# Normalised input of the next attention block: loads and gain products ahead of the block change, high and low parts at it

## The chip, the core and the metric

One core of a Trainium2 chip (trn2). The metric is the device time of one execution in microseconds (us). Engines by the profile's names: PE (TensorE; PEld is its weight load), DVE (VectorE), ACT (ScalarE), POOL (GpSimd) and SP (SyncE), whose queue issues most of the DMAs.

## The reference

One layer with two parallel head groups over 2048 tokens of 1024 features, all in float32:

```python
h = rmsnorm(x, norm_mix_g)             # x * rsqrt(mean(x^2)+eps) * g
proj = h @ w_in                        # columns: u_ssm | q | k | v
y_ssm = s5_mixer(u_ssm, ...)           # complex diagonal scan, GELU, GLU
y_att = chunked_attention(q, k, v, rel_bias)   # 64-frame chunks, 8 to the left
x = x + concat(rmsnorm(y_ssm), rmsnorm(y_att)) @ w_out
x = x + (silu(h2 @ w_gate) * (h2 @ w_up)) @ w_down   # h2 = rmsnorm(x)
return rmsnorm(x)
```

The change concerns `h`, the input of the q, k and v projections.

## The kernel before

The kernel holds activations transposed (features on partitions, tokens on the free axis). Every float32 operand of a product is split into a high part (rounded by a copy to the matmul type `F32R`) and a low part (the rest), and a product is three matmuls: high by high, high by low, low by high (`mm3`, L148).

The run has these stages by the spans of the profile: a prologue with the projection of the scan's input (to about 130 us), attention with the scan beside it (to about 775 us), the output projection, then gate, up and down of the feed-forward part (from about 1000 us to the end).

**Attention** (`att_phase`, L678) works in 4 blocks of 512 tokens (`NSB`, index `sb`). A block is 32 steps: 4 pairs of heads, 2 heads, 4 quarters of 128 queries. A step issues scores of one quarter (`sc`, then the biased row minimum on DVE, L857, and the exponential on ACT, L860), the transposes of the quarter two steps before (`pt`, with their high and low parts `pth` and `ptl`, L875 and L876), every fourth step the product with v (`pj`), and then advances a list of `Unit`s: generators with a first and a last step. The units carry everything else: the projections (`qk_unit`, L740, and `v_unit`, L790, with their results in `pf` and weights in `w`, three buffers), the scan (`ssm_unit`, L557), and the preparation of `h` for the next block (`hT_unit`, L710). With `g0 = 32 * sb` the first step of a block, `CUT` has the first projection of block `sb` begin at `g0 - 8`, and the last one of the block before, `qk_unit(sb - 1, 3)`, ends there. I call that point the block change; there are three.

**`hT_unit`** makes, for each of the 8 feature tiles `q`, the product of the loaded `x` with the gain (a scalar per partition) and with the reciprocal root of the token (`rsn`): L735, on DVE. Then come the high part (L736, a cast on ACT) and the low part (L737, on DVE). Tiles 0 to 2 have two sets of high and low buffers, the `x` in names such as `hi0x` marks the set of odd blocks. Tiles 3 to 7 have one set, so that their high parts can be written only when the last projection of the block before has read the old ones. Tiles 0 to 3 are loaded into `xt` (two buffers), tiles 4 to 7 in two pairs into `raw` (two buffers). In block 0 `raw` also takes the weights before they are split (L686 and L156); the split weights are stored to `wss` (L708) and read back by later blocks (L702).

Before the change, a first unit does tiles 0 to 2 from step `g0 - 12` to `g0 - 9`, its loads up to 2 steps earlier (`HTA`); a second does tiles 3 to 7, all three operations, from `g0 - 8` to `g0 - 6`, its loads 2 steps earlier (`HTS`, `HTP`).

**What sets the order.** PE's instructions stay in program order. On the other engines, SP's queue included, the framework's scheduler places the instructions when the program is built, by priorities and its own idea of durations; after that every engine works strictly in its list's order. So an operation can stand far from where the units put it.

**The scan** shares the stage. `ssm_unit` loads `U`, `Bst`, `Tm` and `Vm` (L564), multiplies `U` by `Bst` on PE (`pj`, copied out at L588), runs a chain of small operations on POOL (L602 to L605, then the carries L613 and L614), hands the states over by four DMAs on POOL's queue (`XG<-X`, L636), and PE multiplies `U` by `Tm` and `XG` by `Vm`. Its results go out at L649. There are 8 such groups. The other DMAs on SP that matter here are q and k copies (L779, L780, L785, L751), bias rows (L552, L553) and the attention output (L910).

At the end of a projection of q and k in block 0, DVE multiplies by the root (L770), ACT makes high parts (L777 for q, L782 for k) and DVE low parts (L778 for q, L783 for k).

Of the kernel before, what the change touches and what calls it, by code (L numbers as in the profile page):

```python
# [13 lines left out]
ALU = mybir.AluOpType  # L14
# [4 lines left out]
KT = D // P  # L19
# [8 lines left out]
NSB = SEQ // SB  # L28
# [9 lines left out]
SGB = 2  # L38
RA1, RA2 = 2, 12
QS = 4, 5, 6, 7, 0, 1, 2, 3  # L40
HTA = -12, -9
HTS = -8, -6
HTP = 2
PRO = 0, 0, 2, 2, 2, 2, 0, 0, 0
LIGHT = 0.8
SL = 1
# [2 lines left out]
DB, XB = 3, 2  # L49
# [47 lines left out]
def f32(ap):  # L97
    return ap.bitcast(F32)
# [302 lines left out]
def u_phase(k, ident, S, aw):  # L401
# [3 lines left out]
    with ExitStack() as cx:  # L405
# [113 lines left out]
        for n in range(1, NSB):  # L519
            last, b = BLOCKS[n - 1 : n + 1]  # L520
            prep(b)
            if n == 1:
                bias_corners(k, S["nba"])
                bias_rows(k, S, 0, S["nba"])
            pf = FBANKS[n]
            now = [group(b, 0, 0 in pf)]
            finish(last, held)
            long(1)
            if n == NSB - 1:
                att = att_phase(k, ident, S, aw, X[b], lambda: ST[b])  # L530
                next(att)
            for f in (1, 2):
                now.append(group(b, f, f in pf))
                if n > 1:
                    long(1)
            sums(b)
            held = now + [group(b, 3, 3 in pf)]
# [140 lines left out]
def att_phase(k, ident, S, aw, x0, roots):  # L678

    tc, nc, io, pfs = k.tc, k.nc, k.io, k.pfs  # L680
    with ExitStack() as cx:
# [28 lines left out]
        def hT_unit(sb, q0=0, q1=KT):  # L710
            hi, lo = hT.setdefault(sb, ([], []))
            ts = slice(sb * SB, (sb + 1) * SB)
            xts = {}

            def load(q, n=1):
                t = k.t(aw, "raw", [P, 1024], bufs=2) if n > 1 else k.t(aw, "xt", [P, SB], bufs=XB)
                nc.sync.dma_start(t[:].rearrange("p (q t) -> p q t", q=n), io["xt"][q * P : (q + n) * P, ts].rearrange("(q p) t -> p q t", p=P))
                for m in range(n):
                    xts[q + m] = t[:, m * SB : (m + 1) * SB]

            if q0 == 0:
                load(0)
                load(1)
            else:
                load(q0)
                for q in range(q0 + 1, q1, 2):
                    load(q, 2)
            for q in range(q0, q1):
                yield
                if q0 == 0 and q + 2 < q1:  # L730
                    load(q + 2)
                xt = xts[q]
                for v, n in zip(hT[sb], ("hi", "lo")):
                    v.append(k.t(aw, f"{n}{q}x" if q < DB and sb % 2 else f"{n}{q}", [P, SB], F32R)[:])
                nc.vector.scalar_tensor_tensor(xt, xt, k.gm[:, q : q + 1], S["rsn"][:, ts], op0=ALU.mult, op1=ALU.mult)  # L735
                nc.scalar.copy(hi[q], xt)  # L736
                nc.vector.tensor_tensor(lo[q], xt, f32(hi[q]), op=ALU.subtract)  # L737
            yield

        def qk_unit(sb, pr):  # L740
# [47 lines left out]
        QK_N = 1 + 2 * KT  # L788
# [142 lines left out]
        sp = tc.alloc_tile_pool(name="ssm", reuse_waits="tile", bufs=1)  # L931
        psum = cx.enter_context(tc.tile_pool(name="aps", bufs=1, space=bass.MemoryType.PSUM, reuse_waits="tile"))
        psum2 = cx.enter_context(tc.tile_pool(name="aps2", bufs=1, space=bass.MemoryType.PSUM, reuse_waits="tile"))
        units = []
        for sb in range(NSB):
            g0 = sb * 32
            C = CUT if sb < NSB - 1 else CUTL
            if sb > 0:
                if DB:
                    units.append(Unit(hT_unit(sb, 0, DB), 2 + DB, g0 + HTA[0], g0 + HTA[1], 2))  # L940
                units += [Unit(hT_unit(sb, DB), 2 + KT - DB, g0 + HTS[0], g0 + HTS[1], HTP), Unit(qk_unit(sb, 0), QK_N, g0 + C[0], g0 + C[1], 3, light=LIGHT)]
            units.append(Unit(v_unit(sb, 0), V_N, g0 + C[1], g0 + C[2], 2, light=LIGHT) if sb else Unit(v0, V_N, *V0, done=1))
            for gen, n, c in ((qk_unit(sb, 1), QK_N, 2), (qk_unit(sb, 2), QK_N, 3), (v_unit(sb, 1), V_N, 4), (qk_unit(sb, 3), QK_N, 5)):
                units.append(Unit(gen, n, g0 + C[c], g0 + C[c + 1], 2, light=LIGHT) if sb else Unit(gen, n + 1, C[c], C[c + 1], 4, light=LIGHT, mid=2))
# [772 lines left out]
```

## Time and profile before

| | |
|---|---|
| median of 3 runs | 2294.59 us (2293.13 to 2301.24) |
| the profiled execution | 2293.41 us, its span 2291.6 us |
| PE busy | 2172.1 us (95% of the span) |
| DVE, ACT, POOL busy | 1542.1, 1000.9, 359.2 us (67%, 44%, 16%) |
| mean granted PE clock | 0.978 |
| around the first block change (130 to 280 us) | PE busy 117.27 of 150 us, clock 0.90 |
| rest of attention (280 to 775 us) | PE busy 450.73 of 495 us, clock 0.96 |
| from 1000 us on | PE busy 1265.88 of 1292 us, clock 0.99 |

A row of the waits view reads "engine, line, releaser: us in total, times, longest us". A row of the timeline reads "start us, duration us, engine, line, operation, out<-in, count", and in brackets the idle time of that engine just before and what ended it. A row of the view by windows has the window, its length, then for PE, PEld, DVE, ACT and POOL the busy us and the instructions, the granted PE clock, the mean share of time in which the 16 DMA engines were busy, and GB/s.

### The profile page before, as it was taken

The numbers are of one execution on the slowest core, as the hardware profiler recorded it, in microseconds if no ns is written. First come the engines' busy times: TensorE is split into PE (matmuls) and PEld (weight loads), VectorE is DVE, ScalarE is ACT, GpSimd is POOL, SyncE is SP. The second block draws the span as 40 slices with busy tenths as digits, with TensorE's granted clock in tenths as the row PEclk, the third lists the DMA queues.
The fourth block names the chain that finished last, engine by engine and source line by source line (L and its number), as shares of the span: only waits on it lengthen the run. The fifth ranks groups of instructions, "written<-read, shape, count | busy, mean of one in ns | idle before, by whom it ended". The sixth has DMA issues, their size and how long they took to land.

```text
span 2291.6 us, 30320 instructions
## 1 busy us (share of the span) xinstructions
PE 2172.1 (95%) x10632; PEld 1828.7 (80%) x10632; DVE 1542.1 (67%) x2695; ACT 1000.9 (44%) x1654; POOL 359.2 (16%) x827
## 2 busy tenths in 40 slices
PE   8987799989987899999999999999999999999997
PEld 6776688888986688878888887888888878888886
DVE  7745565555545855876776668666656477788776
ACT  6445555455546652343333335333333343354322
POOL 2246645456641000000000000000000010000000
PEclk9999999999998999999999999999999999999999
DMA  8766777766644434854564557564423295465552
GB/s 292 241 219 225 227 236 193 190 181 191 191 120 143 161 111 146 284 176 145 162 200 165 198 184 261 184 198 161 167 87 121 84 397 196 165 212 193 207 188 74
DMA packets 214872, 428.34 MB, mean 187 GB/s; under 512 B 38848, under 2 KB 61424, under 8 KB 207616
## 3 DMA queue, kind: packets, MB, share of 16 engines
q1 hardware_dynamic: 207072, 401.49, 54.2%
q0 software_dynamic: 7648, 24.92, 3.2%
q8 instruction: 83, 1.36, 0.2%
q14 instruction: 69, 0.57, 0.1%
HBM read 286.86 MB, written 129.00 MB: 181 GB/s over the span
## 4 chain that ended last, share of the span: by engine, by line
PE 73%; POOL 8%; issue 6%; DVE 4%; DMA 3%; ACT 2%; SPq 1%; DVEq 0%; POOLq 0%; ACTq 0%
PE X L79 20%; PE ps L79 17%; PE Y L79 10%; PE big L79 9%; PE pf L79 5%; PE W L79 5%; PE pj L79 3%; POOL X L605 2%; POOL st L602 1%; POOL st L603 1%; POOL X L604 1%; POOL X L614 1%; POOL fx L613 1%; PE sc L79 1%; PE pt L82 1%
## 5 line engine op out<-in xcount | busy, mean ns | idle before, releaser
L79 PE MATMUL X<-hi,c 128*128 128x512 f32 x1408 | 451.6, 391 | 7.7 <-DVE c L156 5.4
L79 PE MATMUL ps<-hd,hd 128*128 128x512 f32 (+1 forms) x1968 | 428.2, 379 | 3.2 <-DVE hd L156 2.0
L79 PEld LDWEIGHTS ps<-hd,hd 128*128 128x128 f32 x1968 | 356.4, 188 | 73.4 <-DVE hd L156 2.7
L79 PEld LDWEIGHTS X<-hi,c 128*128 128x128 f32 x1408 | 265.6, 189 | 64.0 <-DVE c L156 6.3
L79 PE MATMUL X<-lo,c 128*128 128x512 f32 x704 | 275.1, 391 | 0.0
L156 ACT CAST hd<-hd 128x1536 fp32r<-128x1536 f32 (+1 forms) x106 | 147.3, 1394 | 232.8 <-DMA hd<-hq 165.5
L79 PE MATMUL Y<-hi,c 128*128 128x512 f32 x704 | 225.1, 390 | 1.9 <-DVE u L1396 1.9
L156 DVE TENSOR_TENSOR hd<-hd 128x1536 fp32r<-128x1536 f32 (+1 forms) x106 | 174.1, 1644 | 35.0 <-ACT hd L156 34.5
L156 DVE TENSOR_TENSOR c<-S,c 128x512 fp32r<-128x512 f32 x176 | 121.0, 688 | 100.6 <-ACT c L156 100.3
L1500 POOL DMA_DIRECT2D hd<-hq x7 | 5.3, 764 | 1133.4 <-PE X L79 1121.1
L1392 ACT COPY u<-X 128x512 f32<-128x512 f32 x132 | 77.5, 588 | 201.4 <-PE X L79 201.4
L156 ACT CAST c<-S 128x512 fp32r<-128x512 f32 x176 | 109.4, 622 | 119.8 <-PE Y L79 61.6
L79 PE MATMUL big<-m,woh 128*128 128x512 f32 x512 | 161.0, 396 | 0.0
L1534 DVE TENSOR_TENSOR acc<-acc,ps 128x512 f32<-128x512 f32 x196 | 130.4, 683 | 41.6 <-PE ps L79 41.4
L79 PEld LDWEIGHTS Y<-hi,c 128*128 128x128 f32 x704 | 132.8, 189 | 30.5 <-DVE u L1396 2.8
L79 PEld LDWEIGHTS X<-lo,c 128*128 128x128 f32 x704 | 132.9, 189 | 27.7
L79 PE MATMUL pf<-hi,w 128*128 128x512 f32 x416 | 150.1, 412 | 4.0 <-ACT hi L736 4.0
L156 ACT CAST c<-raw 128x512 fp32r<-128x512 f32 x132 | 82.3, 623 | 151.4 <-PE Y L79 68.5
L79 PE MATMUL Y<-lo,c 128*128 128x512 f32 x352 | 137.3, 390 | 0.0
L876 DVE TENSOR_TENSOR ptl<-pt,pth 128x640 fp32r<-128x640 f32 (+3 forms) x152 | 98.3, 647 | 45.9 <-ACT pth L875 44.4
L860 ACT ACTIVATE s<-s,mn 128x640 f32<-128x640 f32 (+4 forms) x128 | 98.0, 765 | 58.5 <-DVE mn L857 53.6
L875 ACT CAST pth<-pt 128x640 fp32r<-128x640 f32 (+3 forms) x152 | 83.8, 551 | 87.4 <-PE pt L82 82.5
(443 smaller groups left out, 4290.3 us busy)
## 6 DMA issues: line engine op xcount, KB each, us to landing
w<-wss SPq DMA_DIRECT2D x36, 1024.0 KB, 6.3
hq<-g SPq DMA_DIRECT2D x140, 256.0 KB, 2.1
hd<-hq SPq DMA_DIRECT2D x35, 768.0 KB, 4.4
hd<-wc SPq DMA_DIRECT2D x35, 768.0 KB, 5.9
raw<-in_w_gate SPq DMA_DIRECT2D x44, 512.0 KB, 3.7
raw<-in_w_up SPq DMA_DIRECT2D x44, 512.0 KB, 4.2
wc<-px SPq DMA_DIRECT2D x66, 256.0 KB, 3.4
wss<-w SPq DMA_DIRECT2D x12, 1024.0 KB, 4.9
```

The lines of the kernel that those rows point to most:

```text
L79: return self.tc.keep_in_program_order(self.tc.nc.tensor.matmul(*a, **b))
L82: return self.tc.keep_in_program_order(self.tc.nc.tensor.transpose(*a, **b))
L156: return nc.scalar.copy(hi, raw), nc.vector.tensor_tensor(lo, raw, f32(hi), op=ALU.subtract)
L602: eng.tensor_tensor(t[:, :, :, :n], src, ar, op=ALU.mult)
L603: eng.tensor_tensor(t2[:, :, :, :n], src[:, ::-1], aw, op=ALU.mult)
L604: eng.tensor_tensor(dst, dst, t[:, :, :, :n], op=ALU.add)
L605: eng.tensor_tensor(dst, dst, t2[:, :, :, :n], op=ALU.add)
L860: nc.scalar.activation(s[:, :nk], s[:, :nk], AF.Exp, bias=mn[:], scale=-1.0, accum_out=sums[sb, pr][:, hh, qp : qp + 1])
L875: nc.scalar.copy(pth[:, a:b, qp, :], pt[:, a:b, :])
L876: nc.vector.tensor_tensor(ptl[:, a:b, qp, :], pt[:, a:b, :], f32(pth[:, a:b, qp, :]), op=ALU.subtract)
L1392: nc.scalar.copy(u[:], ps[:])
L1534: V.tensor_tensor(a, a, ps[:], op=ALU.add)
```

## The change

The loads and the gain product of tiles 3 to 7 become a first half of `hT_unit(sb, 3)`, spread over steps `g0 - 13` to `g0 - 8` (`HTN`, loads one step earlier, so from `g0 - 14`). The second half, with the high and low parts alone, keeps `HTS`. Both halves are one generator, of which the first unit takes 6 pieces by `islice`. The unit of tiles 0 to 2 keeps its three operations but moves from `g0 - 12 .. g0 - 9` to `g0 - 16 .. g0 - 13`. Lines behind L720 move down: the product is L722, the high part L742, the low part L743, and the later lines of attention stand 6 further.

```diff
-HTA = -12, -9
+HTA = -16, -13
 HTS = -8, -6
-HTP = 2
+HTN = -13, -8
...
+            def norm(q):
+                nc.vector.scalar_tensor_tensor(xts[q], xts[q], k.gm[:, q : q + 1], S["rsn"][:, ts], op0=ALU.mult, op1=ALU.mult)
...
                 for q in range(q0 + 1, q1, 2):
                     load(q, 2)
+                for q in range(q0, q1):
+                    yield
+                    norm(q)
             for q in range(q0, q1):
                 yield
-                if q0 == 0 and q + 2 < q1:
-                    load(q + 2)
-                xt = xts[q]
+                if q0 == 0:
+                    if q + 2 < q1:
+                        load(q + 2)
+                    norm(q)
...
-                nc.vector.scalar_tensor_tensor(xt, xt, k.gm[:, q : q + 1], S["rsn"][:, ts], op0=ALU.mult, op1=ALU.mult)
-                nc.scalar.copy(hi[q], xt)
-                nc.vector.tensor_tensor(lo[q], xt, f32(hi[q]), op=ALU.subtract)
+                nc.scalar.copy(hi[q], xts[q])
+                nc.vector.tensor_tensor(lo[q], xts[q], f32(hi[q]), op=ALU.subtract)
...
+        hts = {sb: hT_unit(sb, DB) for sb in range(1, NSB)}
...
-                units += [Unit(hT_unit(sb, DB), 2 + KT - DB, g0 + HTS[0], g0 + HTS[1], HTP), Unit(qk_unit(sb, 0), QK_N, g0 + C[0], g0 + C[1], 3, light=LIGHT)]
+                units += [Unit(islice(hts[sb], 1 + KT - DB), 1 + KT - DB, g0 + HTN[0], g0 + HTN[1], 1), Unit(hts[sb], 1 + KT - DB, g0 + HTS[0], g0 + HTS[1]), Unit(qk_unit(sb, 0), QK_N, g0 + C[0], g0 + C[1], 3, light=LIGHT)]
```

What the scheduler makes of it: PE's and POOL's orders are the same but for buffer numbers. On DVE, ACT and SP the order changes at the first block change (block 0 to 1), and by a few places in the middle of block 1 (the early tiles of block 2). At the second and third block change only numbers differ: there the loads and products of tiles 3 to 7 stood well ahead of the change already.

Place 1 is DVE at the first block change, where the last projection of block 0 ends. `yt<-pf,rsn` is the root product of k, the `k_...` rows are k's low parts, on which the next scores of PE depend; the rows with `sc` are the score minima, `lo...` low parts of `h` for block 1. Before, from the last early product to k:

```order
L735 SCALAR_TENSOR_TENSOR xt_2599<-xt_2599,g_mix_86,rsn_92 128x512
L857 ISA s_2730,mn_2731<-sc_2727,nbb_1549 128x512
L857 ISA mn_2731 128x1
L876 TENSOR_TENSOR ptl_2687<-pt_2734,pth_2686 128x128
L737 TENSOR_TENSOR lo2x_2648<-xt_2599,hi2x_2647 128x512
L886 RECIPROCAL rs_2893<-sm_2369 128x8
L876 TENSOR_TENSOR ptl_2687<-pt_2734,pth_2686 128x128
L770 TENSOR_TENSOR yt_2750<-pf_2640,rsn_92 128x512
L783 TENSOR_TENSOR k_539_2535<-yt_2750,k_539_2535 64x512
L783 TENSOR_TENSOR k_542_2538<-yt_2750,k_542_2538 64x512
```

and now, where `lo_601` to `lo_626` are the tiles 3 to 7:

```order
L743 TENSOR_TENSOR lo_603_2796<-raw_2510,hi_602_2795 128x512
L863 ISA s_2734,mn_2735<-sc_2731,nbb_1549 128x512
L863 ISA mn_2735 128x1
L882 TENSOR_TENSOR ptl_2696<-pt_2738,pth_2695 128x128
L892 RECIPROCAL rs_2893<-sm_2373 128x8
L882 TENSOR_TENSOR ptl_2696<-pt_2738,pth_2695 128x128
L743 TENSOR_TENSOR lo_605_2800<-raw_2510,hi_604_2799 128x512
L776 TENSOR_TENSOR yt_2754<-pf_2653,rsn_92 128x512
L743 TENSOR_TENSOR lo_607_2804<-raw_2512,hi_606_2803 128x512
L743 TENSOR_TENSOR lo_626_2860<-raw_2512,hi_625_2859 128x512
L789 TENSOR_TENSOR k_549_2558<-yt_2754,k_549_2558 64x512
L789 TENSOR_TENSOR k_552_2561<-yt_2754,k_552_2561 64x512
```

The early product has left this place, and the five low parts of tiles 3 to 7 have come in, four of which stand ahead of k's low parts in these rows (the first, `lo_601`, is the row just above). Before, those five and the five products of their tiles stood 9 rows and more behind k's low parts.

Place 2 is ACT at the same point: `s` the exponential of the scores, `rb` the spread of the row sums, `k` the high parts of k, `hi...` high parts of `h` for block 1. Before:

```order
L736 CAST hi2x_2647<-xt_2599 128x512
L860 ACTIVATE s_2730,sm_2369<-s_2730,mn_2731 128x512
L875 CAST pth_2686<-pt_2734 128x128
L888 COPY rb_2895<-rs_2893 128x512
L782 CAST k_539_2535<-yt_2750 64x512
L782 CAST k_542_2538<-yt_2750 64x512
```

and now:

```order
L866 ACTIVATE s_2734,sm_2373<-s_2734,mn_2735 128x512
L881 CAST pth_2695<-pt_2738 128x128
L742 CAST hi_604_2799<-raw_2510 128x512
L742 CAST hi_606_2803<-raw_2512 128x512
L742 CAST hi_625_2859<-raw_2512 128x512
L894 COPY rb_2895<-rs_2893 128x512
L788 CAST k_549_2558<-yt_2754 64x512
L788 CAST k_552_2561<-yt_2754 64x512
```

Three casts of `h` (tiles 5 to 7) now stand ahead of `rb` and k; tiles 3 and 4 stand a few rows higher. Before, all five came behind the next two quarters' scores.

Place 3 is SP's queue in the 45 us ahead of the first block change: `raw<-in_w_qk` are the last weights of block 0, `wss<-w` stores of split weights, `w<-wss` weights of block 1's first projection, `y<-X` the results of the scan's first group, `U`, `Bst`, `Tm` and `Vm` the loads of its second group. Before, from the last store of weights to the second load of weights:

```order
L708 DMA wss_74<-w_2436 128x2048
L564 DMA Bst_2562<-bsts_70 128x512
L702 DMA w_2652<-wss_74 128x2048
L649 DMA y_65<-X_2491 16x4x256 x8
L910 DMA ya_s_66<-ya_2278 128x512
L564 DMA U_2553<-u_64 16x16x64 x8
L564 DMA Tm_2564<-kts_78 16x4x128 x8
L564 DMA Vm_2573<-vs_71 128x4x128
```

with the early tile `xt_2599`, the four q copies and `w_2654` behind. Now the same stretch, in two pieces; first ahead of the stores of `y`:

```order
L717 DMA xt_2403<-in_xt 128x512
L553 DMA nbb_1549<-nbs_69 64x576
L717 DMA xt_2508<-in_xt 128x512
L717 DMA raw_2510<-in_xt 128x2x512
L717 DMA raw_2512<-in_xt 128x2x512
L708 DMA wss_74<-w_2452 128x2048
```

and then behind them:

```order
L649 DMA y_65<-X_2514 16x4x256 x8
L916 DMA ya_s_66<-ya_2278 128x512
L564 DMA U_2577<-u_64 16x16x64 x8
L564 DMA Bst_2586<-bsts_70 128x512
L564 DMA Tm_2588<-kts_78 16x4x128 x8
L564 DMA Vm_2597<-vs_71 128x4x128
L785 DMA q2h_2556<-q2h_2556 64x512
L786 DMA q2l_2557<-q2l_2557 64x512
L785 DMA q2h_2559<-q2h_2559 64x512
L786 DMA q2l_2560<-q2l_2560 64x512
L702 DMA w_2661<-wss_74 128x2048
L702 DMA w_2663<-wss_74 128x2048
```

All loads of `h` for block 1 now stand ahead of the stores of `y`; the first load of weights for block 1 (`w_2661`) has moved from ahead of them to behind the q copies, and `Bst` from ahead of them to behind the eight loads of `U`.

## The prediction

> **What bounds the kernel now.** Nearly everything is PE: it is busy for 95% of the span, so a change to preparation can only win where PE stands still. I read the waits of PE first, around the first block change (165 to 300 us).
>
> ```profile
> PE pj L79 <- DMA XG<-X: 8.4, 1, 8.4
> PE pt L82 <- DVE ptl L876: 7.0, 6, 3.2
> PE pf L79 <- ACT hi L736: 4.0, 2, 3.1
> PE sc L79 <- issue: 3.9, 1, 3.9
> PE pj L79 <- DMA Tm<-kts: 1.9, 1, 1.9
> PE pf L79 <- DVE lo L737: 1.5, 2, 1.2
> ```
>
> Only the L736 and L737 rows, 5.5 us, are waits for `h`. (The `ptl` row is softmax's own.) They belong to this block change alone: over the whole span the same two rows read the same, number for number. What PE waits for at the other two changes is the low part of k:
>
> ```profile
> PE sc L79 <- DVE k L783: 4.1, 2, 2.2
> ```
>
> Then PE's timeline at the first change, for the places where it stands:
>
> ```profile
> 247.96 0.45 PE L79 MATMUL sc<-k,q2h 128*128 128x128 f32 x1 [3.93 <-issue]
> ...
> 248.93 0.78 PE L79 MATMUL pf<-hi0x,w 128*128 128x512 f32 x1
> ...
> 256.12 0.49 PE L79 MATMUL pf<-hi,w 128*128 128x512 f32 x1 [3.12 <-ACT hi L736]
> ```
>
> Four stops stand in a row: the scan's hand-over at 210 to 218 and its next loads at 235 (the XG and Tm rows above), k at 248, the new `h` from 253 on. The stop called "issue" is k: DVE's low parts of k start at 247.18 (row below), the first of the two ends 0.8 later, and the scores start at 247.96.
>
> The stops cost twice, because the granted clock falls behind them. By windows, with PE's busy time as the second number and the clock after POOL's column:
>
> ```profile
> 256.00:260.00 4.00, 2.02 (x4) 0.77 (x4) 3.90 (x5) 1.74 (x4) 3.84 (x6) 0.76 1.00 341
> 260.00:264.00 4.00, 3.54 (x9) 2.96 (x10) 3.28 (x5) 0.81 (x2) 3.69 (x9) 0.50 0.04 17
> 264.00:268.00 4.00, 4.00 (x24) 3.50 (x23) 2.28 (x6) 2.15 (x5) 3.37 (x16) 0.89 0.01 2
> ```
>
> At clock c, a busy time b would have been b times c at full clock. The loss is 2.02 x 0.24 + 3.54 x 0.50 + 4.00 x 0.11 = 2.7 us.
>
> **The change, part by part.** I take each term in PE's time, against the profiled execution (2293.41 us, of which 2291.6 us is its span; 1.2 us under the median of 2294.59).
>
> *The waits for `h` go.* Loads and products of tiles 3 to 7 move ahead of the change, and the casts and low parts now follow right behind the last reads of the old tiles, near 240 to 247 us by the order, when PE still waits for k. PE needs tile 3 only after 253. So 5.5 us of waiting and 2.7 us of slow clock go: **-8.2 us**. This is the certain part; what follows asks what is late next.
>
> *The k stop.* The same casts and low parts now stand ahead of k on ACT and DVE.
>
> ```profile
> 242.93 1.03 DVE L735 SCALAR_TENSOR_TENSOR xt<-xt,g_mix,rsn 128x512 f32<-128x512 f32 x1 [2.60 <-DMA xt<-in_xt]
> ...
> 245.81 0.68 DVE L770 TENSOR_TENSOR yt<-pf,rsn 128x512 f32<-128x512 f32 x1
> 247.18 1.60 DVE L783 TENSOR_TENSOR k<-yt,k 64x512 fp32r<-64x512 f32 x2 [0.69 <-ACT k L782]
> ```
>
> ```profile
> L736 ACT CAST hi<-raw x12: 604/617/621, 257.8 to 547.3; 128x512 fp32r<-128x512 f32 x12
> ```
>
> Before, DVE sat 2.60 us for a late load, then did 1.03 of product and a low part before it reached `yt` at 245.81, though PE's last product for it ended at 244.03 (247.96 - 3.93). Now DVE has, from 244.03, to wait 0.6 for the cast of tile 5, then does its low part, `yt`, two more low parts and the first k, some 0.69 each: 0.6 + 4 x 0.69 + 0.7 = 4.1 us, against 3.93. **+0.2 us**. The ends: -1.0 (the product was the delay, and the low parts hide in waits for ACT) and +1.9 (the three casts at 0.617 stand wholly in k's way). I take the sum by the rows.
>
> *The first weights of block 1* are no longer fetched at 209.73 but in the place of the second ones:
>
> ```profile
> 209.73 0.72 SPq L702 DMA_DIRECT2D w<-wss  x1
> ...
> 241.84 0.54 SPq L702 DMA_DIRECT2D w<-wss  x1
> ```
>
> The two loads of this stretch took this long from issue to landing:
>
> ```profile
> DMA to landing us min/median/max: 5.8/7.1/8.3
> ```
>
> 241.84 + 7.1 = 248.9, and the first product wants them at 248.93, or 249.8 with the two delays of 0.7 and 0.2 that I count here. **0 us**, from 0 (5.8) to +0.5 at 8.3 (250.1). The second weights are wanted one projection half later.
>
> *`Bst` behind eight loads of `U`.* Before, it was fetched 20 us ahead; the stop at 235 waited for the loads of `U`. Now it comes one place behind the last `U`, which is one issue of SP, some 0.5 us (0.54 in the row of 241.84), later, and is larger (KB each, then median us to landing):
>
> ```profile
> U<-u SPq DMA_DIRECT2D x64, 64.0 KB, 3.0
> ...
> Bst<-bsts SPq DMA_DIRECT2D x8, 256.0 KB, 3.9
> ```
>
> So the wait grows by 0.5 if it lands as fast as `U`, by 0.5 + 0.9 = 1.4 at the medians. DMAs are less busy there than on the mean; I take **+0.7 us**.
>
> *The first hand-over of the scan* (the stop of 8.4 us). POOL ends its chain at 211.3 us and the DMAs carry `XG`; their landing times in that window, and at the next hand-over, were
>
> ```profile
> DMA to landing us min/median/max: 2.3/4.6/6.6
> ```
>
> ```profile
> DMA to landing us min/median/max: 4.1/6.1/7.8
> ```
>
> Two things move. First, POOL is slowed while DVE reads two operands from SBUF:
>
> ```profile
> 206.26 1.06 POOL L614 TENSOR_TENSOR X<-X,fx 128x434 f32<-128x434 f32 x1
> ...
> 209.41 1.90 POOL L614 TENSOR_TENSOR X<-X,fx 128x434 f32<-128x434 f32 x1
> ```
>
> ```profile
> 208.81 1.60 DVE L156 TENSOR_TENSOR w<-raw,w 128x1024 fp32r<-128x1024 f32 x1
> ```
>
> The weight split of 1.60 us cost POOL 0.84. The order puts two products and two low parts of the early tiles (four of about 0.7 us) into POOL's last 8 us: 2.8 x 0.84 / 1.60 = +1.5 us. Second, the 1 MB of weights and `Bst` that were issued just ahead of the last `XG` are replaced by 1 MB in two `raw` loads; the last `XG` may then land as fast as the fastest, 6.6 - 2.3 = 4.3 us earlier, or no earlier at all. I take the two as balancing: **0 us**, from -4.3 to +1.5.
>
> The Trainium skill speaks against the change here: "SBUF — State Buffer", section "Who interferes with whom", has DVE instructions with two SBUF inputs lock out a GpSimd instruction that reads SBUF for their whole length. By it the four operations delay the hand-over by all of their 2.8 us, not 1.5, and the sum below would be -3.8 instead of -6.6. The POOL row above bears out the contention, but at 0.84 for 1.60 us, not one for one.
>
> *The second hand-over.* PE would come to it earlier:
>
> ```profile
> 285.35 1.21 POOL L636 DMA_DIRECT2D XG<-X  x2 [0.30 <-POOL X L614]
> ```
>
> ```profile
> 297.05 0.59 PE L79 MATMUL pj<-XG,Vm 128*128 128x256 f32 x2
> ```
>
> Now PE arrives at 297.05 and does not wait. It will arrive at 297.05 - 8.2 + 0.2 + 0.7 = 289.75. The chain behind `XG` starts from the loads at 235, so it moves by +0.7 alone; but it gets relief, since the block of products and low parts goes that keeps DVE busy for 3.90 of 4.00 us in the window from 256. A scan step on POOL, from one L602 to the next, took
>
> ```profile
> 252.81 0.47 POOL L602 TENSOR_TENSOR st<-X,a 128x128 f32<-128x128 f32 x1
> ...
> 254.87 0.88 POOL L602 TENSOR_TENSOR st<-X,a 128x128 f32<-128x128 f32 x1
> ...
> 261.79 0.56 POOL L602 TENSOR_TENSOR st<-X,a 128x16 f32<-128x16 f32 x1
> ```
>
> 2.06 us once and 6.92 for the next two: 2.8 us lost, of which I give back 0.5 for the low parts that now come at 245 to 247. The last `XG` was issued at 285.35 + 0.6; it will be 285.95 + 0.7 - 2.3 = 284.35, and lands 6.1 later at 290.45. PE waits **+0.7 us**. The ends: 0 if it lands in 4.1, and +4.7 with no relief and 7.8 (294.45).
>
> *The other two block changes:* order and waits the same, **0 us**, 0.5 either way for the few rows that moved inside block 1. Behind 300 us, POOL's chains, loads and hand-overs start from PE's own instructions, so the whole shift stays.
>
> The sum: -8.2 + 0.2 + 0 + 0.7 + 0 + 0.7 + 0 = **-6.6 us**, and 2293.41 - 6.6 = 2286.8 us.
>
> The clock term could be figured otherwise. "TensorE: Matmul & The Clock Gate", section "What's actually happening", in the Trainium skill, gives about 3.4 us of half clock after an idle window. One such period is an estimate of 1.7 us instead of my 2.7, so -5.6 in all; the rows above show more than 4 us at half clock, because the waits kept interrupting.
>
> **The rivals.**
>
> *The second hand-over takes it back.* For: the gain arises behind the point from which POOL's chain starts, and `XG` had landed between 289.4 and 293.8 by the rows. Against: the relief. With the wait of 4.7: -6.6 + 4.0 = -2.6, 2290.8 us.
>
> *The first hand-over gains too.* For: the weights' megabyte and `Bst` leave its way. Against: `raw` loads and the same store of split weights come instead. At -4.3: 2282.5 us.
>
> *Slower, by the scan.* POOL held for the full 2.8 us, and `XG` in a queue of loads at 8.3 instead of 6.6 (+1.7): the first hand-over is 4.5 us late; `Bst` adds 1.4; the chain has no relief and lands after 7.8, at 285.95 + 5.9 + 7.8 = 299.65 instead of being there before 297.05. Then PE loses 2.6 us, 2296.0 us. It decides from where delays less relief and landing exceed 297.05 - 285.95 = 11.1 us; by the rows taken above they are 4.5.
>
> *The stop only moves.* The change touches one block change of three, and even there the scores wait for k behind five casts and low parts (+1.9), then for weights (+0.5): -6.6 + 2.2 = -4.4, 2289.0 us; and if the k stop grew by what the `h` waits lose, nothing would be left. For: three casts and four low parts now precede k in the lists. Against: DVE is rid of a 2.60 us wait there.
>
> **How the numbers follow.** The forecast, -4 to -9, has 0.60; the second hand-over 0.15; the first one earlier 0.12; slower by the scan 0.08; the stop that moves 0.05. The range from 2281.0 to 2293.0 holds the forecast, the second hand-over, the moved stop and most of the first one earlier, and leaves out the slower case; its ends are the unknown first hand-over (-4.3) with a faster k (-1.0), and a second hand-over at its worst with k at its worst. 0.5% is 11.5 us, about what a measurement of this kernel can tell from no change. Faster by more than that needs the first hand-over and k at their good ends: 0.06. Slower by more: 0.02, the far end of the scan's case. Within: 0.92.
>
> **What would show it.** In the changed profile the wait of `pf` for the high and low parts of `h` should be gone, the stop behind the last projection of block 0 should stay near 4 us and end with k's low part, the clock from 256 us on should be full, and PE should come to the second hand-over about 7 us earlier with a wait of a us or so. Wrong: a wait of PE for `w<-wss`, a first hand-over outside 216 to 220 us, a k stop above 5 us, a second hand-over with over 3 us, or changed waits at the second and third block change.

## Result and the profile after

Before and after were timed in turns on the same chips: 2293.40 us before (median of 14 runs, 2288.73 to 2301.24), 2287.02 us after (14 runs, 2281.13 to 2291.83). The ratio is 0.9969, with a 95% interval from 0.9958 to 0.9981: **6.4 us less, 0.3%**. A second set of runs gave 0.9969 again (0.9955 to 0.9984), and the kernel before against itself 1.0004 (0.9989 to 1.0019). So the gain is real, though no larger than the spread of single runs. The forecast was 2286.8 us. Its sum was right; how the sum came about was not, as the traces show.

The profiled execution of after is its fastest run: 2281.13 us, 12.3 less than the profile of before. Behind 300 us two profiles of one kernel drift apart by several us (two of the kernel before by 2.6 at 300 us and 5.1 at 490 us), so I compare places, not spans. PE's waits between 165 and 300 us, in the view "engine, line, releaser: us in total, times, longest":

```profile
PE pt L82 <- DVE ptl L882: 6.2, 5, 3.2
PE sc L79 <- issue: 4.7, 1, 4.7
PE pj L79 <- DVE ptl L882: 4.7, 2, 3.2
PE pj L79 <- DMA XG<-X: 2.6, 1, 2.6
PE pj L79 <- DMA Tm<-kts: 2.0, 1, 2.0
```

The rows of `pf` for high and low parts are gone. But two more rows changed that the forecast had left nearly alone: XG fell from 8.4 to 2.6, and `pj` now waits for `ptl`. On PE's timeline after, the number in brackets is the idle time ahead:

```profile
213.24 0.67 PE L79 MATMUL pj<-XG,Vm 128*128 128x256 f32 x2 [2.58 <-DMA XG<-X]
...
231.70 2.04 PE L79 MATMUL pj<-U,Bst 128*128 128x256 f32 x4 [2.02 <-DMA Tm<-kts]
...
246.46 0.45 PE L79 MATMUL sc<-k,q2h 128*128 128x128 f32 x1 [4.67 <-issue]
...
286.67 0.69 PE L79 MATMUL pj<-ptl,v 128*128 128x384 f32 x1 [3.20 <-DVE ptl L882]
```

The `ptl` that PE waits for at 286.67 stands on DVE behind two products for block 2, which wait for their load (DVE's and SP's timelines):

```profile
284.53 1.62 DVE L722 SCALAR_TENSOR_TENSOR xt<-xt,g_mix,rsn 128x512 f32<-128x512 f32 x2 [4.39 <-DMA xt<-in_xt]
286.06 0.55 DVE L882 TENSOR_TENSOR ptl<-pt,pth 128x384 fp32r<-128x384 f32 x1
```

```profile
275.61 1.01 SPq L717 DMA_DIRECT2D xt<-in_xt  x2
```

These are the early tiles of block 2, some 115 us ahead of their use (PE's first product of block 2 starts at 390.50): their loads are issued at 275.61, and DVE's products start 8.9 us later.

**How far PE is ahead, place by place.** The scores `sc<-k,q2h` come in the same order in all kernels. For each I took the start of the same score row in two profiles; the difference to before is the shift. Its change over a stretch is what the stretch won (-) or lost (+), slow clock included. The stretches, by the times of before: A, 206 to 231, the first hand-over; B, 231 to 241, the stop for U, Tm and Bst; C, 241 to 252, the k stop; D, 252 to 267, the tiles of the new `h`; E, 291.7 to 299.9, the second hand-over. Each row is one profile.

| us | A | B | C | D | E |
|---|---|---|---|---|---|
| forecast | 0 | +0.7 | +0.2 | -8.2 | +0.7 |
| after | -2.9 | +1.7 | +1.5 | -8.5 | +4.1 |
| after, second profile | -3.8 | +3.9 | +0.8 | -8.8 | +2.8 |
| before, second profile | -0.4 | -0.1 | +0.8 | +1.2 | 0.0 |
| 1 early tiles only | -2.4 | -0.3 | -3.0 | +0.3 | 0.0 |
| 2 split products only | -1.1 | -0.3 | -0.5 | +0.5 | -0.7 |
| 3 two transfers back | -2.2 | -0.2 | -0.4 | -2.5 | -0.3 |
| 4 products behind ptl | -2.0 | +3.4 | +1.5 | -8.4 | +1.3 |
| 5 block 2 loads in order | -1.0 | +1.7 | +1.5 | -8.4 | -0.7 |
| 6 k first | -5.3 | +4.2 | -1.3 | -8.8 | +3.4 |
| 7 Bst first | -5.6 | +0.9 | +1.5 | -8.3 | +4.2 |
| 8 = 5 + 6 + 7 | -5.7 | +2.9 | -1.3 | -8.8 | +3.9 |
| 9 = 5 + 6 | -2.5 | +1.7 | -1.4 | -8.7 | +6.1 |
| 10 = 9, one weight load back | -3.1 | +3.1 | -1.3 | -8.8 | +0.1 |

### The profile page after: what moved, and what is told of

It reads as the page before. It is cut to its first block, busy times and chain, and to the rows that moved or that the text cites. A ratio compares the mean times of both kernels' runs of the same rounds, so it can differ in the third digit from the quotient of the medians.

```text
span 2279.4 us, 30314 instructions
## 1 busy us (share of the span) xinstructions
PE 2170.2 (95%) x10632; PEld 1828.3 (80%) x10632; DVE 1541.6 (68%) x2695; ACT 999.2 (44%) x1654; POOL 353.7 (16%) x827
## 4 chain that ended last, share of the span: by engine, by line
PE 65%; POOL 11%; issue 8%; DMA 7%; DVE 5%; ACT 2%; SPq 1%; POOLq 0%; DVEq 0%; ACTq 0%
PE X L79 20%; PE ps L79 17%; PE Y L79 10%; PE big L79 7%; PE W L79 5%; PE pf L79 3%; POOL X L605 2%; DMA acc<-x 2%; POOL X L604 2%; POOL X L614 2%; POOL st L602 2%; POOL fx L613 2%; POOL st L603 2%; PE pj L79 1%; DMA lo<-hc 1%
## 5 line engine op out<-in xcount | busy, mean ns | idle before, releaser
L882 DVE TENSOR_TENSOR ptl<-pt,pth 128x640 fp32r<-128x640 f32 (+3 forms) x152 | 98.2, 646 | 44.8 <-ACT pth L881 43.2
```

Of the source, the lines that this page charges most:

```text
L882: nc.vector.tensor_tensor(ptl[:, a:b, qp, :], pt[:, a:b, :], f32(pth[:, a:b, qp, :]), op=ALU.subtract)
```

## Experiments

The theory after reading the two traces: D is the change's own gain and belongs to the whole change; A comes from the DMAs beside the last XG; E is DVE's stand for the load of block 2. The rivals: A is POOL's chain or chance; E is the second hand-over itself, so that XG ends it whatever DVE does.

**Second profiles of both kernels** (no edit) separate chance from change.

> The changed kernel itself once more, for a second profile. By the theory three things recur to 0.5 us: no wait of pf for high and low parts of h, DVE's stand of 4.4 us ahead of the products at 280 to 285 with PE's wait of 3.2 us for ptl, and the stop ahead of the scores of block 1 of 4.7 us. Open is the first hand-over of the scan, where PE's wait fell from 8.4 to 2.6 and the shift went from -1.0 to -4.0 us: if the changed loads make it, it recurs (-3 against before); if it was the chance of POOL's chain that began 1.75 us earlier in that execution, the second profile has the wait at 4 to 8 us.

> The kernel before once more, for a second profile and as a measure of how far the comparison itself scatters: ratio 1.000 within 0.0015. Open is the first hand-over: four profiles of changed kernels have PE's wait for XG at 1.1 to 3.5 us against 8.4 in the one profile of before. If that is the change, 7 to 9 us recur here, with XG issued last near 211.6 and landed 6 us later; if the profile of before was the exception, 2 to 5 us are seen here.

All three local findings recurred: no wait for `h`, a stop of 4.71 us at k, and 3.26 us of PE for `ptl`. The wait for XG recurred too, 3.0 us after against 8.7 before. So the shorter wait in A is the work of the change. The second profile of before also says what it isn't (POOL's last XG issues, SP's load, and PE's row):

```profile
209.32 1.21 POOL L636 DMA_DIRECT2D XG<-X  x2 [0.30 <-POOL X L614]
```

```profile
209.35 0.55 SPq L702 DMA_DIRECT2D w<-wss  x1
```

```profile
218.00 1.19 PE L79 MATMUL pj<-XG,Vm 128*128 128x256 f32 x2 [8.70 <-DMA XG<-X]
```

POOL was 2.3 us earlier here than in the first profile (209.32 against 211.60), and PE went on at 218.00 instead of 218.44. POOL does not set this hand-over. XG lands 7.5 us after its last issue ended (218.00 - 209.32 - 1.21), beside 1 MB of weights issued at the same moment. Here and below, XG counts as landed when PE starts its first product, which waits for it.

The size of A is another matter: in the nine profiles of kernels with the whole change it reaches from -1.0 to -5.7. It goes with how long the clock stayed at half, by the clock records of the traces. Half clock lasted 10.24 us in this stretch in both profiles of before and in 5 (-1.0), 6.83 us in after, 4, 9 and 10 (-2.0 to -3.1), 3.41 us in the second profile of after, 6 and 8 (-3.8 to -5.7), and in 7 (-5.6) there was none. Experiment 2, whose wait for XG stayed, has -1.1 with 6.83 us. So about 1 us of A can come without any gain at XG.

**1. The early tiles alone**

An edit of the kernel before:

```diff
-HTA = -12, -9
+HTA = -16, -13
```

> The kernel before with one of the two halves of the change: the first three tiles of each block loaded and multiplied four steps sooner; tiles 3 to 7 as before. Theory: the waits for h belong to tiles 3 to 7, so they stay at 4 to 5.5 us with the slow clock behind them, and nothing of the 8.5 us is won between 252 and 263. The first hand-over of the scan gains only if the weight split and the weight load leave its way: by the order both stand where the changed kernel has them, so PE's wait for XG falls from 8.4 to about 3 us and the shift behind it is -3 to -5, of which the stops at 232 and 247 give back 2 to 4. In all 0 to -3 us, ratio 0.9987 to 1.000. Rival: the first hand-over gain needs the whole change (or was chance in the profile of before), then the wait for XG stays at 7 to 8 us.

0.9980 (0.9966 to 0.9993). Its waits:

```profile
PE pf L79 <- ACT hi L736: 3.5, 2, 3.1
PE pj L79 <- DMA XG<-X: 3.0, 1, 3.0
PE sc L79 <- issue: 2.5, 1, 2.5
```

As expected, D stays (+0.3) and A comes (-2.4): SP now issues `w<-wss` at 212.14, behind the last XG at 209.58, which lands 4.0 us after its issue ended. Not expected was C: the k stop fell from 3.93 to 2.52, for the third early tile's late load is out of DVE's way. POOL's and DVE's last rows ahead of the hand-over look alike here and in after. Those of after show that the two slow each other:

```profile
206.81 1.38 POOL L614 TENSOR_TENSOR X<-X,fx 128x434 f32<-128x434 f32 x1
```

```profile
205.58 1.71 DVE L743 TENSOR_TENSOR lo0x<-xt,hi0x 128x512 fp32r<-128x512 f32 x1
```

The low part took 1.71 us (0.69 where it stands alone), and POOL's row 1.38, where the weight split of before made it 1.90.

**2. The split products alone**

An edit of the changed kernel:

```diff
-HTA = -16, -13
+HTA = -12, -9
-HTN = -13, -8
+HTN = -9, -8
```

> The other half of the change alone: products of tiles 3 to 7 in steps of their own ahead of their casts and low parts, with every unit's time as in the kernel before (the first three tiles four steps later than in the changed kernel, the products from nine steps ahead of the block). Theory: what removes the waits for h is that loads and products stand ahead of k; with the old times the order puts them behind k as before, so PE's waits for hi and lo stay at 4 to 5.5 us, the first hand-over keeps its 8 to 9 us (the first weights of block 1 are loaded ahead of XG as before), and the time is that of before within 1.5 us, ratio 0.9993 to 1.0007. Rival: splitting alone lets the casts follow sooner, and 3 us or more of the waits for h go.

0.9996 (0.9984 to 1.0008), and the waits are those of before:

```profile
PE pj L79 <- DMA XG<-X: 8.2, 1, 8.2
...
PE pf L79 <- ACT hi L742: 3.9, 2, 3.1
PE sc L79 <- issue: 3.6, 1, 3.6
PE pf L79 <- DVE lo L743: 2.5, 2, 2.1
```

The split is worth nothing by itself; with the old times the products stay behind k in DVE's order, and so do the casts.

**3. Two transfers kept behind the first hand-over**

An edit of the kernel before; `keep_in_program_order` sets the order of issue alone:

```diff
-nc.sync.dma_start(f32(w[:]), S["ws"][n])
+ins = nc.sync.dma_start(f32(w[:]), S["ws"][n])
+if (sb, n) == (1, 0):
+    tc.keep_in_program_order(ins)
...
-nc.sync.dma_start(S["ws"][n], f32(keep.pop(n)[:]))
+ins = nc.sync.dma_start(S["ws"][n], f32(keep.pop(n)[:]))
+if n == 7:
+    tc.keep_in_program_order(ins)
```

> The kernel before, with two transfers of 1 MB each (the first weights of block 1 and a store of split weights) kept behind the first hand-over on SP; by the order one load of 0.5 MB for tiles 4 and 5 takes their place ahead of it. Nothing else of the change. Theory: the first hand-over of before is late since XG lands 6 to 8 us after its last issue, behind the 1 MB load issued at 209.4 to 209.7; with half of those bytes ahead it lands 1.5 to 4 us sooner, PE's wait falls from 8.4 to 4 to 7 us, and the shift behind it is -1.5 to -4 us, of which the later stops keep about half. Rival: the wait is POOL's chain and DVE beside it, which stay; then PE's wait for XG stays at 8 to 9 us and the time is that of before.

0.9968 (0.9955 to 0.9981): the order of a few transfers gave as much as the whole change. The store came later anyway in before (243.58 us); what moved is the load of the weights, and 0.5 MB of tiles took its place. XG landed 4.6 us after its issue ended (214.86 - 209.10 - 1.21) instead of 7.5 and 5.6 (218.44 - 211.60 - 1.21):

```profile
214.86 1.19 PE L79 MATMUL pj<-XG,Vm 128*128 128x256 f32 x2 [6.15 <-DMA XG<-X]
...
252.05 0.79 PE L79 MATMUL pf<-hi,w 128*128 128x512 f32 x1 [3.12 <-ACT hi L740]
```

Against the second profile of before, where POOL's issue came at nearly the same time (209.32), the landing is 2.9 us sooner, and the wait fell by 2.6 (8.70 to 6.15), since PE came 0.6 us earlier. What the expectation missed is D, -2.5: the 0.5 MB that moved up are tiles 4 and 5 of block 1, and only one wait for `h` was left.

**4. The products of block 2 behind ptl**

An edit of the changed kernel; `issue_after` sets the order of issue alone, and `k.last_ptl` is the last subtraction for block 0 (L882):

```diff
 def norm(q):
-    nc.vector.scalar_tensor_tensor(xts[q], xts[q], k.gm[:, q : q + 1], S["rsn"][:, ts], op0=ALU.mult, op1=ALU.mult)
+    with tc.issue_after(k.last_ptl.ins) if sb == 2 and q < 2 else nullcontext():
+        nc.vector.scalar_tensor_tensor(xts[q], xts[q], k.gm[:, q : q + 1], S["rsn"][:, ts], op0=ALU.mult, op1=ALU.mult)
```

> The changed kernel, with DVE's products of the first two tiles of block 2 queued behind the last subtraction ptl of block 0 instead of just ahead of it (issue order alone; the loads stay). Theory: in the changed kernel the shift of PE against before falls from -9.2 us (scores at 273 to 288 us) to -5.2 us (scores at 300 us) since DVE stood 4.39 us for the load of these tiles and ptl came 3.2 us late for PE. Without that the shift stays near -9: 3.2 to 4.0 us less than the changed kernel, ratio to before 0.9952 instead of 0.9969, and no wait of PE for ptl over 1 us at 283 to 287. Rival: the second hand-over of the scan is the limit there; PE then waits 3 to 4 us for XG at 288 to 292 instead, and the time stays within 1 us of the changed kernel.

0.9961 (0.9946 to 0.9976), not told apart from after. The wait for `ptl` is gone; the rival's wait came in its place, but smaller:

```profile
290.86 0.67 PE L79 MATMUL pj<-XG,Vm 128*128 128x256 f32 x2 [0.86 <-issue]
293.02 0.70 PE L79 MATMUL pj<-U,Tm 128*128 128x256 f32 x2 [0.63 <-DVE ya L909]
```

E fell from +4.1 and +2.8 to +1.3. Theory and rival were both half right: DVE's stand is what held PE in after, and XG arrives just behind it.

**5. The loads of blocks 2 and 3 in written order**

An edit of the changed kernel; `ins` is the load of L717:

```diff
+if sb > 1:
+    tc.keep_in_program_order(ins)
```

> The changed kernel, with the loads of the tiles of blocks 2 and 3 kept on SP at their place in the written order; in the changed kernel they run ahead to 275.6 us, 200 us before block 2 begins, where 1.5 MB of them lie beside the second hand-over of the scan, and DVE's products for them move with them. Theory: what the changed kernel gives back between 288 and 300 us are two waits in a row, DVE's stand ahead of ptl and, once that is gone (1.3 us given back instead of 4.0 with the products queued behind ptl), the XG of the second hand-over, which landed 7 to 8 us after its issue. With these loads out of the way both go: no wait of PE for ptl at 283 to 287, XG lands in about 4.7 us as at the first hand-over, PE waits under 1 us for it, and the shift of the scores against before at 300 us stays at -8 to -9 instead of -5 to -6.5. Rival: XG is as late without them, and PE waits 1 to 3 us for it at 288 to 291; the shift at 300 us is then -5 to -7.

0.9957 (0.9940 to 0.9974). E is -0.7: nothing is given back. (The loads had led their use by some 115 us, not by 200.) PE reaches XG without a wait:

```profile
289.66 0.59 PE L79 MATMUL pj<-XG,Vm 128*128 128x256 f32 x2
```

**6. k ahead of tiles 5 to 7**

An edit of the changed kernel; `k.kh` and `k.kl` are the last high and low part of k (L788, L789) that are written ahead:

```diff
-nc.scalar.copy(hi[q], xts[q])
-nc.vector.tensor_tensor(lo[q], xts[q], f32(hi[q]), op=ALU.subtract)
+late = sb == 1 and q >= 5
+with tc.issue_after(k.kh.ins) if late else nullcontext():
+    nc.scalar.copy(hi[q], xts[q])
+with tc.issue_after(k.kl.ins) if late else nullcontext():
+    nc.vector.tensor_tensor(lo[q], xts[q], f32(hi[q]), op=ALU.subtract)
```

> The changed kernel, with the casts and low parts of tiles 5 to 7 of block 1 queued behind the high and low parts of k, which the changed kernel does after them. Theory: PE's stop ahead of the scores of block 1 is made by what stands ahead of k; three low parts (0.93 and twice 0.85) and three casts (1.66) leave its way, ACT's k starts at 242.8 instead of 243.86, DVE's first low part of k ends at 244.3 instead of 246.3, and the stop falls from 4.67 to about 2.5 us: 2 us less than the changed kernel, and no wait for tiles 5 to 7, since PE needs tile 3 only after 251. Rival: k is bound by what ACT and DVE must do anyway (the softmax rows), and the stop stays above 4 us; or the waits for the low parts of h come back with 1 us or more at 252 to 258.

0.9957 (0.9941 to 0.9973). The stop is 2.53 us, as expected, and no wait for `h` came back; softmax's own row then waits 1.46:

```profile
245.27 0.30 PE L79 MATMUL sc<-k,q2h 128*128 128x128 f32 x1 [2.53 <-issue]
249.58 0.36 PE L79 MATMUL sc<-k,q2h 128*128 128x256 f32 x1 [1.46 <-DVE mn L866]
```

So the order "low parts, then k" costs 2.1 us of wait at C, and in after it takes back the gain that experiment 1 shows there.

**7. Bst ahead of U**

An edit of the changed kernel, in `ssm_unit`; the load of `Bst` follows there, unchanged:

```diff
-    for j in range(L):
-        load(U[j * CH : (j + 1) * CH].rearrange("c g (n t) -> c g n t", n=NSB), S["u"].rearrange("(c g) n j t -> c g n j t", c=CH)[:, GB * b : GB * b + GB, :, j])
...
+    for j in range(L):
+        load(U[j * CH : (j + 1) * CH].rearrange("c g (n t) -> c g n t", n=NSB), S["u"].rearrange("(c g) n j t -> c g n j t", c=CH)[:, GB * b : GB * b + GB, :, j])
```

> The changed kernel, with Bst loaded ahead of the eight U instead of behind them. Theory of the prediction: Bst behind U costs 0.7 us of PE's wait (2.0 us in the changed kernel) and slow clock with it, so this gives 0.5 to 1.5 us back, once in the first scan chain, and the wait at 232 ends with U or Tm at about 1 us. Rival: the last of U or Tm is as late as Bst, the wait stays at 2.0 and nothing changes (within 0.3 us); or U is now later by the 0.25 MB ahead of it and the wait grows by 0.5.

0.9977 (0.9964 to 0.9991): no gain over the changed kernel in the whole. At its place B falls from +1.7 and +3.9 to +0.9, but not by the wait, which is 2.83 us and lies between those of the two profiles of after (2.02 and 2.98):

```profile
231.25 1.10 PE L79 MATMUL pj<-U,Bst 128*128 128x256 f32 x4 [2.83 <-DMA Tm<-kts]
```

The clock makes the difference. Windows after the stop, in after and in this run (the clock is the third number from the end):

```profile
229.00:232.00 3.00, 0.98 (x4) 0.54 (x4) 1.86 (x4) 1.26 (x2) 0.00 (x0) 0.94 0.68 160
232.00:235.00 3.00, 3.00 (x8) 2.49 (x8) 0.56 (x2) 1.14 (x4) 0.00 (x0) 0.50 0.61 147
```

```profile
232.00:236.00 4.00, 4.00 (x23) 3.52 (x22) 1.40 (x4) 3.46 (x9) 0.00 (x0) 1.00 0.73 185
```

The last of the recorded rivals fits, that `U` is later by the 0.25 MB ahead of it. The wait itself depends on when PE arrives, so I count from the first store of `y`, which opens this stretch of SP's queue, to PE's product: 10.5 and 10.4 us in the two profiles of before, 11.6 and 11.5 in those of after (`Bst` behind `U`), and 11.4 here (`Bst` ahead of `U`). `Bst` in this stretch goes with 1 us, in either place. That it is `Bst` is argued and not shown: no run here has the whole change with `Bst` fetched 20 us ahead.

**8, 9 and 10: the edits together.** 8 has the edits of 5, 6 and 7, and 9 those of 5 and 6. 10 is 9 with one weight load of block 1 kept in written order:

```diff
-nc.sync.dma_start(f32(w[:]), S["ws"][n])
+ins = nc.sync.dma_start(f32(w[:]), S["ws"][n])
+if (sb, n) == (1, 2):
+    tc.keep_in_program_order(ins)
```

> The changed kernel with three further edits: block 2's loads kept in written order, tiles 5 to 7 behind k, and Bst ahead of U. Theory: the edits add up, since each acts on a stop of its own: 2 to 3 us for Bst, 2 us for k, so -5 us at the first tiles of block 1 (252 us of before) instead of -0.7, -13 us at 290, and XG of the second hand-over issued near 278 us and landed near 283, when PE comes for it at 297.05 - 13.4 = 283.7: the shift at 300 us is -12 to -13, ratio 0.994 to 0.995. Rival: the second hand-over is the limit behind which no gain passes; PE then waits 3 to 5 us for XG at 284 to 289, and the shift at 300 us is -8 to -9, as with k ahead alone.

> The changed kernel with block 2's loads in written order and tiles 5 to 7 behind k, but Bst behind U as in the changed kernel. Theory: the second hand-over of the scan is now the bound, behind which only part of the gain passes; the version with Bst ahead came to it at -13.6 us and left it at -9.8. Here PE comes to it at -9 to -11.5 and leaves it at -8 to -10: 1 to 2 us of wait for XG at 286 to 290, ratio 0.9955 to 0.9965, the same as with Bst ahead, within 1.5 us. Rival: the gains add up, the wait for XG stays under 0.5 us, and the shift at 300 us equals that at 290.

> The version with block 2's loads in written order and tiles 5 to 7 behind k, and one of the two weight loads of 1 MB that SP issues at 278.4 us, ahead of the last two XG at 280.6, kept behind the second hand-over. Theory: both hand-overs of the scan end when XG has come through the DMA queues behind megabyte loads of weights issued a little ahead of it, not with POOL's chain. In the version without this edit PE came to the second hand-over at -11.7 us against before, stood 4.27 us for XG, which landed 7.2 us after its issue had ended at 281.8, and left at -5.6. With 1 MB less ahead of it XG lands 2 to 4 us sooner, the wait falls to 0.5 to 2.5 us and the shift at 300 us is -7.5 to -10; ratio 0.9955 to 0.9975, where the version without it had 0.9984. The load that is moved is used 25 us later and costs nothing, unless it now collides with U and Tm. Rival: POOL's chain ends when it does and XG lands 6 to 8 us later in any case; then the wait stays at 4 us and the shift at 300 us at -5 to -6.

0.9965 (0.9953 to 0.9977), 0.9984 (0.9972 to 0.9995) and 0.9977 (0.9963 to 0.9991): the edits do not add up. In 9, PE comes to the second hand-over at -11.7 us, further ahead than in any kernel but 8, and stands 4.27 us for XG:

```profile
289.02 1.19 PE L79 MATMUL pj<-XG,Vm 128*128 128x256 f32 x2 [4.27 <-issue]
```

The row names no releaser ("issue"); by the landings in the trace the third of the four XG came at 288.93, just ahead of it. The SP rows and POOL rows of 9 there, and then those of 5:

```profile
278.42 1.76 SPq L702 DMA_DIRECT2D w<-wss  x2
```

```profile
280.59 1.21 POOL L636 DMA_DIRECT2D XG<-X  x2 [0.30 <-POOL X L614]
```

```profile
283.50 1.76 SPq L702 DMA_DIRECT2D w<-wss  x2
```

```profile
282.02 1.21 POOL L636 DMA_DIRECT2D XG<-X  x2 [0.30 <-POOL X L614]
```

SP's two weight loads move with PE: PE is 5.1 us earlier in 9 than in 5 (-11.7 against -6.6), and so are the loads (278.42 against 283.50). This puts 2 MB ahead of XG instead of behind it, and XG lands 7.2 us after its issue ended. Experiment 10 took 1 MB of it away: XG was there after 3.5 us (286.70 - 282.03 - 1.21), and E fell from +6.1 to +0.1. The theory of XG among megabytes holds. Its claim that the moved load costs nothing does not:

```profile
286.70 0.67 PE L79 MATMUL pj<-XG,Vm 128*128 128x256 f32 x2 [0.59 <-issue]
...
312.19 0.53 PE L79 MATMUL pf<-hi0x,w 128*128 128x512 f32 x1 [2.32 <-DMA w<-wss]
```

There PE now waits 2.32 us for these weights, and the shift goes from -11.1 to -7.1.

## Why the prediction was right, and where it was not

- **The waits for `h` go, -8.2.** Right, mechanism and size: -8.3 to -8.8 in all nine profiles of kernels that hold the whole change, full clock from 252.2 to 268 us in both profiles of after, and nothing of it with either half alone. (The second profile of before has +1.2 there, so the size is known to about 1 us.)
- **The first hand-over, 0.** Wrong: -2.9 and -3.8. The failed step is "I take the two as balancing". The price of the port fight (+1.5) was not paid by POOL: in after DVE lost 0.86 us in a product (1.61 instead of 0.75) and 1.02 in a low part (1.71 instead of 0.69), POOL 0.32 in its worst row (1.38), which improved when the weight split left its side. The row of 1.90 us that the price came from was also misread: it overlaps the split for 1.00 us (209.41 to 210.41), not for 1.60, and lost 0.84 of that. From its first 128x434 row to the last XG issue POOL took 10.7 us in both profiles of after, and 11.6 and 11.3 in those of before. And the DMA side, put at 0 to -4.3, came: XG lands 3.6 and 4.0 us after its last issue, instead of 5.6 and 7.5. Experiment 3 shows that it needs only the load of the weights to go behind XG. What PE wins by it varies with the clock behind the stop, as said above. This was a rival with a chance of 0.12; its 2282.5 failed since B, C and E took the gain back.
- **`Bst` behind `U`, +0.7.** Mis-sized. The loads came 1.1 us later behind the stores of `y`, within the 0.5 to 1.4 of the sum, and PE's wait grew by 0.1 and 1.1 us (2.02 and 2.98 against 1.88). But B is +1.7 and +3.9 in the two profiles of after, since the clock falls behind the stop. The sum priced slow clock at the `h` waits only. It also took the order against `U` as the cause; experiment 7 shows that ahead of `U` is no better.
- **The k stop, +0.2.** The wait came out at 4.67 us, for 4.1 predicted, which with the clock behind it gave +1.5 and +0.8 at C (the second profile of before has +0.8 there by itself, so the wait's 0.7 is the surer number). Both parts of the sum were real, and larger: rid of the late load the stop is 2.52 us, and tiles 5 to 7 put 2.1 back.
- **The first weights of block 1, 0.** Right: no wait for them in either profile of after.
- **The second hand-over, +0.7.** Mis-sized, +4.1 and +2.8, and of another cause. XG was there. The failed step is the line on the other block changes, "0.5 either way for the few rows that moved inside block 1": among these rows were two products of block 2 that stand on DVE ahead of `ptl` and now came to their load too early. Experiments 4 and 5 show it.
- **The sum, -6.6.** The five stretches sum to -4.1 and -5.1 in the two profiles; A won 2.9 and 3.8 more than forecast, B, C and E lost 5.7 and 5.9 more. PE is 5.2 and 6.6 us ahead at 300 us, of which 1.0 and 1.3 were there at 206 us already. The second profile of before has +1.5 over the same stretches; against it the sums are -5.6 and -6.6. The medians differ by 6.4, and the interval of the ratio reaches from 4.4 to 9.6 us. So the total holds because errors of both signs met, and that is luck. What the kernel gains or loses behind 300 us could not be told from scatter.
- **The rivals.** "The second hand-over takes it back" was not what after shows, but it is the limit just behind: 9 shows it. Of the signs named as wrong, one came (a first hand-over at 213.24 and 213.74, outside 216 to 220 us), and it pointed at the right term. At the second hand-over PE stood over 3 us, but for `ptl` and not for XG. The waits for k at the second and third block change stayed (4.1 us in two waits, the longest 2.2, before and after). "The stop only moves" and "slower by the scan" did not come.

Whether 5 or 6 is better than the changed kernel stays open: the intervals around their 0.9957 (0.9940 to 0.9974) and those around the changed kernel's 0.9969 (0.9955 to 0.9984) overlap in most of their length. No version here is shown to beat it.

## What to carry to other kernels

When a load moves, price it at the transfer that it meets on the way, not only at its own consumer: the first hand-over here, and in experiment 9 the second, was set by megabyte loads that happened to be issued 0 to 2.2 us ahead of a small, urgent transfer. A faster engine frees buffers sooner and so can bring such loads forward by itself. And rows that move "only a few places" need the same look as the moved ones: ask what each waits for and who is queued behind it.

## What the runs showed of the hardware

- At the stop of B, five profiles had waits of 1.62 to 1.88 us, and the clock stayed at 1.00 behind it. Nine had 1.95 to 3.73 us; in eight of them the clock fell to 0.50 for 3.41 or 6.83 us, and in one (2.83 us, experiment 7) it did not. In after, 0.14 us more of wait than before came with a loss of 1.7 us at B. The Trainium skill ("TensorE: Matmul & The Clock Gate", section "What's actually happening") has the clock fall after an idle window of about 3.4 us that runs free. The clock records of the traces agree on the window: from 130 to 775 us, in all 14 profiles, the clock keeps each value for a whole multiple of 3.41 us. But the window need not be idle. Between 140 and 775 us of these profiles, PE was busy for under 1.46 us in 124 of the windows at full clock, and the next window was at half clock in all 124. With 1.60 us or more that came in 7 of 2187 windows, all 7 behind 620 us; between the two values both were seen.
- This sorts the stops of B, the exception too. In the eight that cost clock, the emptiest window had 0.26 to 1.46 us of PE; in the six others it had 1.60 to 2.31. In after, the stop from 229.69 to 231.70 lies in the window from 228.24 to 231.65, with 1.45 us of PE; in before, the one from 233.65 to 235.53 is split by a window's end at 234.19, which leaves 2.87 and 2.08. In experiment 7 the 2.83 us are split at 230.07, which leaves 1.76 and 2.24. So about 1.9 us of standing inside one window was enough here, and where the windows lie differs from run to run. That is a source of the scatter in A, B and C.
- XG, four transfers of 127.5 KB from POOL's queue, landed 3.5 us (10, second hand-over), 3.6 us (after: 213.24 - 208.48 - 1.21), 4.0 us (1) and 4.6 us (3) after the end of its last issue, and 5.6 and 7.5 us (the two profiles of before) and 7.2 us (9, second hand-over). From 4 us ahead of its last two issues to their end SP had issued 0.6 to 1.75 MB in the first four, and 2 to 2.25 MB in the others. POOL's queue does not keep it apart from SP's. "DMA: Bandwidth & Descriptors", section "Issuing engines are not separate DMA queues", in the Trainium skill says the same: transfers of all issuing engines share the same DMA engines and interleave.
- This count does not sort every case. At the second hand-over of after the last XG landed 7.5 us after its issue (280.65 to 288.18 by the landings in the trace) with 1.5 MB counted so, all of it loads of `x`; at the first it had been 4.3 us. In experiment 5, where SP issued nothing in that time, it took 4.8 us (283.23 to 287.98). PE came behind XG in both cases, so that PE's rows do not show it.
